# A gate pair by seven products, a layer norm on ScalarE, and low parts of weights by adding DMAs

## The chip, the core and the metric

The kernel runs on one core of a Trainium2 chip. The time is the device time of one execution in microseconds (us). Five engines work side by side, each through its own instructions in the order in which they were laid down: TensorE (PE, with its weight loads PEld), VectorE (DVE), ScalarE (ACT), GpSimd (POOL) and SyncE (SP, which here only issues DMAs). They wait for one another by semaphores. DMAs are issued by SP, by POOL and a few by ACT.

## The reference

One layer of a hybrid encoder, 512 positions of width 1024, in float32. Cut to what this case touches:

```python
n = rms_norm(h, norm_mix_pre)
proj = n @ w_in                       # columns: u 512 | v 512 | q, k, v 3 x 1536 | gates 2 x 1024
u, v = gelu(proj[:, :512]), gelu(proj[:, 512:1024])
v = (v - mean(v)) * rsqrt(var(v) + eps) * gain + bias           # layer norm over 512 channels
y_a = u * (w_spatial @ v + b_spatial)                           # 4 chunks of 128, 4 groups of channels
y_b = dilated_window_attention(q, k, v)                         # 3 head groups, mixed
g_a, g_b = sigmoid(gates + b_gate)
merged = g_a * (y_a @ w_branch_a) + g_b * (y_b @ w_branch_b)
h = h + rms_norm(merged @ w_out)
h = h + rms_norm(relu(rms_norm(h) @ w_up) ** 2 @ w_down)
```

## The kernel before

**Precision.** Every large product is made in a reduced 32-bit format (float32r). Both operands are split into a high part, which is the value rounded to that format, and a low part, which is what is left; `mm3` then adds high x high, low x high and high x low: three matmuls for one. A split of a weight (`wsplit`, `split_into`) is a copy on ACT for the high part and a subtraction on DVE or POOL for the low part.

**Seven products.** Where a product is large, the kernel uses a scheme in Strassen's manner: from a pair of 128-column weight blocks and two halves of 256 positions it makes seven products of half the contraction and half the positions, each of 4 x 3 = 12 matmuls of 128x256, where the plain way needs 2 x 8 x 3 = 48 matmuls of 128x512. The weights must first be added into sums: `seven` makes three sums on DVE (lines 339, 340, 344), splits them by `wsplit` into s12 and s34, and splits three raw blocks by `split1` (ar0, ar1, a12). The moving side (`nmov`, made early in `four_sums`) is shared by all pairs.

**Order.** The program is traced in the order of the code; a planner then orders each engine's instructions by a simulated timeline, so that instructions of neighbouring parts are interleaved. `tc.issue_after(x)` makes the instructions of a block stand behind x on x's engine. A tile with a single buffer (the pool `gapool` has one of each name) is written again only when its last reader is done.

**The stage around the change**, in the order of the code:

1. After the last attention head's scores, `token_major(COL_V, ...)` projects the gMLP values v by chunks of 128 positions. `evac_v` (line 685 on) takes each chunk from PSUM: GELU (ACT and DVE), `bn_stats` and `bn_aggr` for mean and variance on DVE, the power of -1/2 on POOL (`rstd_of`, line 96), and at line 694 one DVE instruction (v - mean) * r in place. `normed` keeps these instructions.
2. Four groups g of the first half u: the weights come in two loads (`uw`, 1024 KB each); each group is split at line 704 with the subtraction on POOL (`sub=nc.gpsimd`), multiplied (24 matmuls), put through GELU, and joined with the spatial product `pg` (line 719), which reads the normalized v. The last head's attention is interleaved (`attend_steps`).
3. The gates. With `GSTD = 1`, output block d = 0 takes the plain way: lines 793 to 799 split both gate weights and make 2 x 24 matmuls, then a sigmoid each. Blocks 1 to 7 go through `seven_pairs`, whose first `seven` stands behind the last of `normed`. Within a pair the products come as 6, (the tail of the pair before: product 4 and `after`), 1, 5, 2, 7, 3. X takes products 1 and 2, Y 6, 7 and 4, Z 5 and 3; `p1`, `z5`, `u2`, `u3` are copies and sums taken between two products into one bank.
4. `branches(d)`, called for d = 0 and from `gate_after` for the rest: for br = 1 and 0 the 128-column block of `w_branch_b` and `w_branch_a` (loaded to `bw` by SP at line 760) is split into the tile `b1` or `b0`, multiplied in 12 matmuls, and weighed with the gate; then the sum is split into `mh`, `ml` for the product with w_out.

Of the kernel before, what the change touches and what calls it, by code (L numbers as in the profile page):

```python
# [10 lines left out]
F32 = mybir.dt.float32  # L11
F32R = mybir.dt.float32r
AF = mybir.ActivationFunctionType
ALU = mybir.AluOpType
PSUM = bass.MemoryType.PSUM

P = 128
S = 512
D = 1024
KD = D // P  # L20
# [8 lines left out]
COL_U, COL_V = 0, GW  # L29
# [7 lines left out]
def block_kernel(ctx: ExitStack, tc: tile.TileContext, x, norm_mix_pre, w_in, b_gate, ln_v_gain, ln_v_bias,  # L37
                 w_spatial, b_spatial, w_branch_a, w_branch_b, w_out, norm_mix_post, norm_mlp_pre, w_up,
                 w_down, norm_mlp_post, ident_c, rope_c, mask_c, perm_c, out):
    nc = tc.nc  # L40
    x, out, w_in, w_up, w_down, w_out = x[0], out[0], w_in[0], w_up[0], w_down[0], w_out[0]
    w_branch_a, w_branch_b, w_spatial = w_branch_a[0], w_branch_b[0], w_spatial[0]
# [10 lines left out]
    wpool = pool(wstack, "wpool", bufs=3)  # L53
# [15 lines left out]
    def wsplit(raw, pl=None, bufs=None, tag="w", sub=None):  # L69
        pl = pl or wpool  # L70
        shape = list(raw.shape)
        hi = pl.tile(shape, F32R, name="hi", tag=tag + "hi", bufs=bufs)
        lo = pl.tile(shape, F32R, name="lo", tag=tag + "lo", bufs=bufs)
        nc.scalar.activation(hi, raw, AF.Copy)  # L74
        (sub or nc.vector).tensor_tensor(lo, raw, hi.bitcast(F32), op=ALU.subtract)  # L75
        return hi, lo

    def split_into(hi, lo, src, sub=nc.vector):
        nc.scalar.activation(hi, src, AF.Copy)  # L79
        return sub.tensor_tensor(lo, src, hi.bitcast(F32), op=ALU.subtract)  # L80
# [131 lines left out]
    scaled, hi, lo, _ = norm_x(blocks[0], xts[0], rs[0])  # L212
# [12 lines left out]
    for i in range(4):  # L225
        if i + 1 < 4:
            _, hi, lo, turned = norm_x(blocks[i + 1], xts[i + 1], rs[i + 1])
# [34 lines left out]
    A, B = slice(0, 256), slice(256, 512)  # L262
# [39 lines left out]
    def fcols(wap, c0, nk, n, raw=None):  # L302
        return wap[:, c0:c0 + n].rearrange("(k p) c -> p k c", p=P)
# [45 lines left out]
    def product(n, ps, w, moving, first):  # L349
        (wh, wl), (bh, bl) = w[n], moving[n]  # L350
        for j in range(KH):
            for i, (a, b) in enumerate(((wh, bh), (wh, bl), (wl, bh))):
                nc.tensor.matmul(ps, a[:, j], b[:, j], start=first and not (j or i), stop=(j == KH - 1 and i == 2), skip_group_check=True)  # L353

    def seven_pairs(n, weights, moving, banks, snap, two, rows, evac, after):
        tail = None
        for i in range(n):
            c2, c1 = rows(i)
            w = weights(i)
            Y, Z, X = banks()  # L360
            product(6, Y, w, moving, True)
            if tail:
                tail()
            product(1, X, w, moving, True)
            p1, z5, u2, u3 = snap("p1", two), snap("z5", 1), snap("u2", 1), snap("u3", 1)
            nc.scalar.activation(p1, X, AF.Copy)
            nc.vector.tensor_tensor(u2, Y, p1, op=ALU.add)
            product(5, Z, w, moving, True)
            nc.scalar.activation(z5, Z, AF.Copy)
            product(2, X, w, moving, False)  # L370
            evac(i, c1[:, A], X)
            product(7, Y, w, moving, False)
            nc.vector.scalar_tensor_tensor(u3, Y, -1.0, p1, op0=ALU.mult, op1=ALU.subtract)
            product(3, Z, w, moving, False)
            nc.vector.tensor_tensor(c1[:, B], Z, u2, op=ALU.add)
            nc.vector.tensor_tensor(c2[:, B], u3, z5, op=ALU.subtract)

            def tail(i=i, w=w, Y=Y, p1=p1, c2=c2):
                product(4, Y, w, moving, False)
                nc.vector.scalar_tensor_tensor(c2[:, A], Y, -1.0, p1, op0=ALU.mult, op1=ALU.subtract)  # L380
                after(i)
        tail()
# [301 lines left out]
    normed = []  # L684

    def evac_v(c, ps):
        v = vln[:, c]
        gelu2(ps, v)
        st6 = small.tile([P, 6], F32, name="st6")
        nc.vector.bn_stats(st6, v)  # L690
        mv = small.tile([P, 2], F32, name="mv")
        nc.vector.bn_aggr(mv, st6)
        r = rstd_of(mv[:, 1:2], 1.0, 4.0 * EPS)
        normed.append(nc.vector.tensor_scalar(v, v, mv[:, 0:1], r, op0=ALU.subtract, op1=ALU.mult))

    token_major(COL_V, lambda n, k, c: n[:, k, ROT + c * P:ROT + (c + 1) * P], evac_v)

# [2 lines left out]
    for g2 in range(2):  # L700
        raw = wload([KD, 2 * P], lambda r: [(r, fcols(w_in, COL_U + g2 * 2 * P, KD, 2 * P))], "uw")
        for j in range(2):
            g = 2 * g2 + j
            wh, wl = wsplit(raw[:, :, j * P:(j + 1) * P], sub=nc.gpsimd)
            ps = psA.tile([P, S], F32, name="pf", tag="acc" if g else "T", bufs=4 if g else 1)
            for k in range(KD):
                ins = mm3(ps, (wh[:, k], wl[:, k]), (nhn[:, k], nln[:, k]), k == 0, k == KD - 1)
                if k % 4 == 3 and steps:
                    with tc.issue_after(ins.ins):
                        if next(steps, 0) == 0:  # L710
                            steps = None
            u = gpool.tile([P, S], F32, name="u", bufs=2)
            gelu2(ps, u)
            if g == 0:
                with tc.issue_after(ins.ins):
                    spatial_weights()
            pg = psA.tile([P, 4, P], F32, name="pg", tag="acc", bufs=4)
            for c in range(4):
                nc.tensor.matmul(pg[:, c], vln[:, c, g * P:(g + 1) * P], wst[:, g], start=True, stop=True)
            t = gpool.tile([P, 4, P], F32, name="sv")  # L720
            nc.vector.scalar_tensor_tensor(t, pg, cols[:, 16 + g:17 + g], sbias[:, g:g + 1].to_broadcast([P, 4, P]), op0=ALU.mult, op1=ALU.add)
            tf = t.rearrange("p c t -> p (c t)")
            nc.vector.scalar_tensor_tensor(tf, tf, 0.5, u, op0=ALU.mult, op1=ALU.mult)
            split_into(yah[:, g], yal[:, g], tf)
# [8 lines left out]
    gapool = pool(gp, "gapool")  # L733
    gs, rawb = {}, {}

    GSTD = 1

    w7 = w_down.rearrange("(c j h p) d -> c h p j d", p=P, h=2, j=4)
    halves = [slice(0, 512), slice(512, 1024)]
# [11 lines left out]
    def gate_rows(i):  # L751
        d = i + GSTD
        gs[d] = gapool.tile([P, 2, S], F32, name="gs")
        return gs[d][:, 0], gs[d][:, 1]
# [9 lines left out]
    def gate_weights(i):  # L764
        raw = gate_raw(i + GSTD)
        with nullcontext() if i else tc.issue_after(normed[-1].ins):
# [5 lines left out]
    def gate_evac(i, dst, X):  # L772
        d = i + GSTD
        nc.scalar.activation(dst, X, AF.Sigmoid, bias=cols[:, d:d + 1])

    def gate_after(i):
        d = i + GSTD
        nc.scalar.activation(gs[d][:, 1, B], gs[d][:, 1, B], AF.Sigmoid, bias=cols[:, d:d + 1])
# [3 lines left out]
    def branches(d):  # L782
        g = gs.pop(d)
        for br in (1, 0):
            bhl = gapool.tile([P, 2, 4, P], F32R, name=f"b{br}")
            split_into(bhl[:, 0], bhl[:, 1], rawb[d][:, br])
            yh, yl = ((yah, yal), (ybh, ybl))[br]
            pb = feature_tile(bhl[:, 0], bhl[:, 1], 4, yh, yl, "Ty"[br])
            nc.vector.tensor_tensor(g[:, 1 - br], pb, g[:, 1 - br], op=ALU.mult)
        nc.vector.tensor_tensor(g[:, 0], g[:, 0], g[:, 1], op=ALU.add)  # L790
        split_into(mh[:, d], ml[:, d], g[:, 0])

    for d in range(GSTD):
        g2 = gate_rows(d - GSTD)
        raw = gate_raw(d)
# [51 lines left out]
    for k0 in range(0, KD, 2):  # L847
        raw = wload([2, D], lambda r: [(r, w_out[k0 * P:(k0 + 2) * P].rearrange("(k p) c -> p k c", p=P))], "wow")
        for j in range(2):
            wos.append(wsplit(raw[:, j]) if k0 + j < 3 else wsplit(raw[:, j], wopool, tag="wo"))  # L850
    raw = wload([KD, 2 * P], lambda r: [(r, fcols(w_up, 0, KD, 2 * P))], "upw")
# [28 lines left out]
    for t in range(4):  # L880
# [18 lines left out]
        r = rstd_of(ss, 1.0 / D)  # L899
# [30 lines left out]
    def hid_of(f):  # L930
        return hid[f // 8][:, f % 8]
# [10 lines left out]
    for i in range(1, NSTD):  # L942
        raw = raw_up(i)
        for j in range(2):
            wh, wl = split_back(raw[:, :, j * P:(j + 1) * P], [KD, P])
# [13 lines left out]
    A, B = slice(0, 256), slice(256, 512)  # L959
# [37 lines left out]
    moving = {1: nb[0, 0], 2: nb[1, 0], 3: nb[1, 1], 4: nt[4], 5: nt[1], 6: nt[2], 7: nt[3]}  # L997
# [11 lines left out]
    def snap(name, bufs=1):  # L1009
        return upool.tile([P, 256], F32, name=name, bufs=bufs)  # L1010

    tail = None
    for i in range(NSTD, KF // 2):
# [3 lines left out]
        c2, c1 = hid_of(f), hid_of(f + 1)  # L1017
        w = prep(i)
        Y, Z, X = half_bank("acc"), half_bank("acc"), half_bank("tp")
# [3 lines left out]
        p1, z5, u2 = snap("p1", 2), snap("z5"), snap("u2")  # L1023
# [11 lines left out]
        u3 = c2[:, 256:]  # L1035
# [7 lines left out]
        def tail(w=w, Y=Y, p1=p1, c2=c2, f=f):  # L1043
# [13 lines left out]
    X, W, Y, Z = [[accs[t][hf].rearrange("p (b d) -> p b d", d=256) for t in ts]  # L1057
                  for ts, hf in (((0, 1), 0), ((0, 1), 1), ((2, 3), 0), ((2, 3), 1))]
# [50 lines left out]
    for c in range(NC):  # L1109
        h = h_split(a11[c], c == 0)  # L1110
        with ExitStack() as order:
# [3 lines left out]
            w = w_split(pairs(block(c, 0, 0)))  # L1115
# [107 lines left out]
    for t in range(2):  # L1223
        with tc.issue_after(final.ins) if final else nullcontext():
            for j in range(4):
                wh, wl = w[j // 2]
                final = acc3(Y[t], (hh[:, j, tsl[t]], hl[:, j, tsl[t]]), (wh[:, j % 2], wl[:, j % 2]), False, j == 3)
        weighed(Y[t], None, 0, sums[2 + t][:, 1:2])
        r = rstd(2 + t)
# [50 lines left out]
```

## Time and profile before

| | us |
|---|---|
| median of three runs | 778.27 |
| lowest and highest run | 777.62, 779.86 |
| the profiled execution | 779.39 |
| its span, first to last instruction | 777.6 |
| PE busy in the span | 768.1 |
| DVE busy | 606.4 |
| ACT busy | 460.5 |
| POOL busy | 90.6 |

The median is what the change is measured by; the profiled execution is one of its own, with 1.8 us outside the span. Busy time of PE is the union of its matmuls, whose ends are modelled: an instruction's own duration (389 ns for a 128x512 matmul) contains the overlap with the next, and the pace of matmuls is read from the distance of their starts. In a row of the timeline the columns are the start, the duration, engine, line, operation, output<-input, and in brackets the idle time before it with what ended it. The granted clock of PE was 0.998.

### The profile page before, as it was taken

To read this page: it belongs to the slowest core of one execution; us is meant where nothing else is said; L and a number is where in the kernel's file an instruction comes from. 1 tells how busy PE (TensorE), PEld (TensorE's weight loads), DVE (VectorE), ACT (ScalarE), POOL (GpSimd) and SP (SyncE) were. 2 spreads that over 40 slices of the span, in tenths; PEclk is the share of its full clock that TensorE was granted. 3 is DMA by queue.
4 is the path that set the end of the run, shared out by engine and by line. 5 is a ranking of instruction groups with operands and counts; after the bars stand their busy time and mean duration, and the time that the engine had idled before them with its cause. 6 is when DMAs were issued, how large, how long until landed. Compare 5 with 4: busy or idle time off the path is not lost.

```text
span 777.6 us, 12381 instructions
## 1 busy us (share of the span) xinstructions
PE 768.1 (99%) x4859; PEld 693.7 (89%) x4859; DVE 606.4 (78%) x974; ACT 460.5 (59%) x751; POOL 90.6 (12%) x125
## 2 busy tenths in 40 slices
PE   8999999999999999999999999999999999999996
PEld 6888999999998888999998899999999988888885
DVE  6785589888883888868756569998888699978785
ACT  5442558978777546545544457566666766655670
POOL 2301200010103400000000210011211100203010
PEclk9999999999999999999999999999999999999999
DMA  9733844253454633433546414469999988979702
GB/s 299 257 112 108 217 109 109 55 144 101 125 175 84 201 82 83 109 82 105 144 159 203 150 69 147 152 200 285 200 277 220 240 303 312 198 248 215 214 1 109
DMA packets 104749, 128.30 MB, mean 165 GB/s; under 512 B 3265, under 2 KB 75233, under 8 KB 103794
## 3 DMA queue, kind: packets, MB, share of 16 engines
q1 hardware_dynamic: 83920, 83.50, 34.2%
q0 software_dynamic: 20480, 43.61, 23.5%
q8 instruction: 38, 0.62, 0.3%
q10 hardware_dynamic: 290, 0.40, 0.1%
q14 instruction: 21, 0.17, 0.1%
HBM read 117.53 MB, written 26.74 MB: 186 GB/s over the span
## 4 chain that ended last, share of the span: by engine, by line
PE 64%; issue 0%; DVE 0%; ACT 0%; POOLq 0%; POOL 0%; DVEq 0%; ACTq 0%
PE pacc L1003 13%; PE pd L1095 6%; PE pd L1094 6%; PE pd L1096 6%; PE pgacc L353 6%; PE ptp L1003 5%; PE pf L86 3%; PE pf L85 3%; PE pf L84 3%; PE pgS L353 3%; PE pd L84 2%; PE pd L86 2%; PE pd L85 2%; PE pu L85 1%; PE pu L86 1%; PE pu L84 1%
## 5 line engine op out<-in xcount | busy, mean ns | idle before, releaser
L1095 PE MATMUL pd<-hl,hhl 128*128 128x512 f32 x224 | 87.2, 389 | 0.0
L1096 PE MATMUL pd<-hl,hhl 128*128 128x512 f32 x224 | 87.0, 389 | 0.0
L1094 PE MATMUL pd<-hl,hhl 128*128 128x512 f32 x224 | 84.7, 389 | 0.0
L1003 PE MATMUL pacc<-nt,hl 128*128 128x256 f32 x504 | 66.1, 279 | 0.0
L1003 PEld LDWEIGHTS pacc<-nt,hl 128*128 128x128 f32 x504 | 62.0, 188 | 0.1
L74 ACT ACTIVATE hi<-s 128x1024 fp32r<-128x1024 f32 x32 | 33.8, 1058 | 29.5 <-DVE s L340 7.9
L1096 PEld LDWEIGHTS pd<-hl,hhl 128*128 128x128 f32 x224 | 42.1, 188 | 8.8
L1094 PEld LDWEIGHTS pd<-hl,hhl 128*128 128x128 f32 x224 | 42.0, 188 | 8.8
L1095 PEld LDWEIGHTS pd<-hl,hhl 128*128 128x128 f32 x224 | 42.0, 188 | 8.6
L75 DVE TENSOR_TENSOR lo<-s,hi 128x1024 fp32r<-128x1024 f32 x32 | 39.1, 1223 | 10.0 <-ACT hi L74 9.8
L80 DVE TENSOR_TENSOR hl<-dnw,hl 128x1024 fp32r<-128x1024 f32 x32 | 38.4, 1222 | 8.6 <-ACT hl L79 8.6
L79 ACT ACTIVATE hl<-s 128x1024 fp32r<-128x1024 f32 x28 | 29.4, 1057 | 26.1 <-DVE s L986 18.8
L79 ACT ACTIVATE hl<-dnw 128x1024 fp32r<-128x1024 f32 x32 | 33.0, 1053 | 19.3 <-DMA dnw<-in_w_down_dram 10.1
L1003 PE MATMUL pacc<-n,hl 128*128 128x256 f32 x336 | 44.1, 279 | 0.0
L1003 PEld LDWEIGHTS pacc<-n,hl 128*128 128x128 f32 x336 | 41.4, 188 | 0.0
L353 PE MATMUL pg<-nt,hi 128*128 128x256 f32 x216 | 39.8, 281 | 0.0
L80 DVE TENSOR_TENSOR hl<-s,hl 128x1024 fp32r<-128x1024 f32 x28 | 34.2, 1221 | 5.2 <-ACT hl L79 5.2
L84 PE MATMUL pf<-nh,hi 128*128 128x512 f32 x96 | 37.9, 395 | 0.0
L86 PE MATMUL pf<-nh,lo 128*128 128x512 f32 x96 | 37.7, 393 | 0.0
L85 PE MATMUL pf<-nl,hi 128*128 128x512 f32 x96 | 37.7, 392 | 0.0
L85 PE MATMUL pv<-lo,nh 128*128 128x512 f32 x96 | 37.5, 391 | 0.0
L84 PE MATMUL pv<-hi,nh 128*128 128x512 f32 x96 | 37.2, 394 | 0.0
(385 smaller groups left out, 2274.6 us busy)
## 6 DMA issues: line engine op xcount, KB each, us to landing
upw<-in_w_up_dram SPq DMA_DIRECT2D x16, 1024.0 KB, 6.2
qkw<-in_w_in_dram SPq DMA_DIRECT2D x24, 512.0 KB, 5.2
dnw<-in_w_down_dram SPq DMA_DIRECT2D x12, 1024.0 KB, 6.9
gw<-in_w_in_dram SPq DMA_DIRECT2D x16, 512.0 KB, 5.2
t3d<-in_w_down_dram POOLq DMA_DIRECT2D x8, 1024.0 KB, 8.9
t1d<-in_w_down_dram POOLq DMA_DIRECT2D x8, 1024.0 KB, 9.3
slab<-in_w_in_dram SPq DMA_DIRECT2D x6, 1024.0 KB, 12.5
tsum<-in_w_down_dram POOLq DMA_DIRECT2D x6, 1024.0 KB, 9.7
```

Of the source, the lines that this page charges most:

```text
L74: nc.scalar.activation(hi, raw, AF.Copy)
L75: (sub or nc.vector).tensor_tensor(lo, raw, hi.bitcast(F32), op=ALU.subtract)
L79: nc.scalar.activation(hi, src, AF.Copy)
L80: return sub.tensor_tensor(lo, src, hi.bitcast(F32), op=ALU.subtract)
L84: nc.tensor.matmul(ps, ah, bh, start=start, stop=False)
L85: nc.tensor.matmul(ps, ah, bl, start=False, stop=False)
L86: return nc.tensor.matmul(ps, al, bh, start=False, stop=stop)
L353: nc.tensor.matmul(ps, a[:, j], b[:, j], start=first and not (j or i), stop=(j == KH - 1 and i == 2), skip_group_check=True)
L1003: ins = nc.tensor.matmul(ps, a[:, j], b[:, j], start=first and not (j or m), stop=(j == KH - 1 and m == 2), skip_group_check=True)
L1094: nc.tensor.matmul(ps, ah, bh, start=start, stop=False, skip_group_check=True)
L1095: nc.tensor.matmul(ps, ah, bl, start=False, stop=False, skip_group_check=True)
L1096: return nc.tensor.matmul(ps, al, bh, start=False, stop=stop, skip_group_check=True)
```

## The change

Four edits.

- `GSTD` becomes 0: block d = 0 also goes through `seven_pairs` (eight pairs instead of seven), and the loop of the plain way is empty.
- `seven_pairs`: in the first pair, which has no tail of a pair before it, the order of the products becomes 1, 2, 6, 5, 7, 3, with the bank X emptied after product 2. The other pairs keep theirs.
- `evac_v`: the instruction (v - mean) * r on DVE is replaced by a negation of the mean (128x1, DVE) and two activations over the chunk on ACT, v - mean and then times r. `normed` now keeps the negations.
- A new helper `dma_split` is used for the four gMLP first-half weights and the sixteen branch weights: the high part by a copy on ACT, then the negated high part into the low tile by a second copy on ACT, then a DMA issued by POOL that adds the weight itself, from DRAM, to that tile. It replaces the subtraction (on POOL for the first, on DVE for the second).

```diff
+    def dma_split(raw, src, hi=None, lo=None):
+        if hi is None:
+            hi = wpool.tile(list(raw.shape), F32R, name="hi", tag="whi")
+            lo = wpool.tile(list(raw.shape), F32R, name="lo", tag="wlo")
+        nc.scalar.activation(hi, raw, AF.Copy)
+        nc.scalar.activation(lo, hi.bitcast(F32), AF.Copy, scale=-1.0)
+        nc.gpsimd.dma_start(lo, src, accum_op=ALU.add)
         return hi, lo
...
             Y, Z, X = banks()
-            product(6, Y, w, moving, True)
+            p1, z5, u2, u3 = snap("p1", two), snap("z5", 1), snap("u2", 1), snap("u3", 1)
             if tail:
+                product(6, Y, w, moving, True)
                 tail()
             product(1, X, w, moving, True)
-            p1, z5, u2, u3 = snap("p1", two), snap("z5", 1), snap("u2", 1), snap("u3", 1)
             nc.scalar.activation(p1, X, AF.Copy)
+            if not tail:
+                product(2, X, w, moving, False)
+                evac(i, c1[:, A], X)
+                product(6, Y, w, moving, True)
             nc.vector.tensor_tensor(u2, Y, p1, op=ALU.add)
             product(5, Z, w, moving, True)
             nc.scalar.activation(z5, Z, AF.Copy)
-            product(2, X, w, moving, False)
-            evac(i, c1[:, A], X)
+            if tail:
+                product(2, X, w, moving, False)
+                evac(i, c1[:, A], X)
...
-        normed.append(nc.vector.tensor_scalar(v, v, mv[:, 0:1], r, op0=ALU.subtract, op1=ALU.mult))
+        normed.append(nc.vector.tensor_scalar(mv[:, 0:1], mv[:, 0:1], -1.0, None, op0=ALU.mult))
+        nc.scalar.activation(v, v, AF.Identity, bias=mv[:, 0:1])
+        nc.scalar.activation(v, v, AF.Copy, scale=r)
...
-            wh, wl = wsplit(raw[:, :, j * P:(j + 1) * P], sub=nc.gpsimd)
+            wh, wl = dma_split(raw[:, :, j * P:(j + 1) * P], fcols(w_in, COL_U + g * P, KD, P))
...
-    GSTD = 1
+    GSTD = 0
...
-            split_into(bhl[:, 0], bhl[:, 1], rawb[d][:, br])
+            dma_split(rawb[d][:, br], fcols((w_branch_a, w_branch_b)[br], d * P, 4, P), bhl[:, 0], bhl[:, 1])
```

More of the change, by code (lines that the diff above doesn't have):

```diff
@@ L75, in wsplit @@
         (sub or nc.vector).tensor_tensor(lo, raw, hi.bitcast(F32), op=ALU.subtract)
+        return hi, lo
+    def dma_split(raw, src, hi=None, lo=None):
[5 more added lines that the diff above has]
+        nc.gpsimd.dma_start(lo, src, accum_op=ALU.add)
         return hi, lo
```

## The prediction

> **What bounds the kernel.** I read the page's busy times first, then the chain of waits, then the waits of PE alone.
>
> ```profile
> PE 768.1 (99%) x4859; PEld 693.7 (89%) x4859; DVE 606.4 (78%) x974; ACT 460.5 (59%) x751; POOL 90.6 (12%) x125
> PE 64%; issue 0%; DVE 0%; ACT 0%; POOLq 0%; POOL 0%; DVEq 0%; ACTq 0%
> ```
> ```profile
> PE pt L192 <- DVE w0lo L207: 1.9, 1, 1.9
> PE idle L160 <- POOL neghalf L60: 1.0, 1, 1.0
> ```
>
> PE is busy 99% of the span, the chain holds nothing else of weight, and PE's two listed waits (2.9 us) lie at the kernel's start. The stage of the change, in windows (length, then busy time of PE, PEld, DVE, ACT, POOL; clock; DMA share):
>
> ```profile
> 265.00:275.00 10.00, 9.89 (x58) 8.33 (x57) 9.26 (x18) 2.14 (x3) 2.76 (x3) 1.00 0.41 120
> 275.00:285.00 10.00, 10.00 (x50) 8.43 (x49) 8.34 (x12) 3.96 (x6) 0.00 (x0) 1.00 0.03 6
> 285.00:290.00 5.00, 5.00 (x27) 4.28 (x27) 4.16 (x6) 2.07 (x3) 0.00 (x0) 1.00 1.13 299
> 355.00:371.00 16.00, 16.00 (x115) 15.02 (x114) 12.70 (x20) 8.18 (x15) 0.00 (x0) 1.00 0.44 115
> ```
>
> The reader is to see PE filled to the last digit, except for 0.11 us at 265 to 275, at full clock. So time falls only by fewer matmuls or by that 0.11 us; work taken from DVE or POOL is worth nothing by itself. And time rises by every hole that a late operand makes.
>
> **Part 1, block 0 by seven products.** Two pairs of rows of PE's timeline give the pace of each way: the first matmul of block 0 and the first after it; the last product 4 of the stage and the first matmul after it.
>
> ```profile
> 286.54 0.48 PE L84 MATMUL pf<-nh,hi 128*128 128x512 f32 x1
> 297.51 0.40 PE L353 MATMUL pgacc<-nt,hi 128*128 128x256 f32 x2
> ...
> 409.73 1.56 PE L353 MATMUL pgacc<-nt,ar 128*128 128x256 f32 x12
> 411.14 0.39 PE L84 MATMUL pd<-hi,mh 128*128 128x512 f32 x1
> ```
>
> The plain way takes 297.51 - 286.54 = 10.97 us for 48 matmuls. A product takes 411.14 - 409.73 = 1.41 us, so seven take 9.87. Gain: **1.10 us**. That is all PE can win here, 0.14% of the time.
>
> What it adds is DVE work: two splits of 1024 columns go, the sums, two splits of sums and three splits of raw blocks come.
>
> ```profile
> L75 DVE TENSOR_TENSOR lo<-gw,hi x2: 1215/1216/1217, 275.4 to 282.2; 128x1024 fp32r<-128x1024 f32 x2
> L339 DVE TENSOR_TENSOR s<-gw x7: 1218/1225/1226, 270.9 to 372.4; 128x1024 f32<-128x1024 f32 x7
> L340 DVE TENSOR_TENSOR s<-s,gw x7: 680/685/695, 272.2 to 374.5; 128x512 f32<-128x512 f32 x7
> L80 DVE TENSOR_TENSOR ar<-gw,ar x14: 682/689/694, 296.7 to 395.2; 128x512 fp32r<-128x512 f32 x14
> ```
>
> New for block 0: 1.22 + 2 x 0.69 (sums) + 2 x 1.22 + 3 x 0.69 (splits) = 7.1 us, less 2 x 1.22 = 2.4 of the plain way: 4.7 us more, wanted between the last normalization (270.5) and about 292, where product 7 would start (286.5 + 4 x 1.41). DVE's idle time from 275 to 290 is 1.66 + 0.84 = 2.5 us, and part 2 frees about 2 us more, so the work fits, barely. Product 1 wants only ar0, and product 2 only a12, neither of them a sum; this is what the new order of the first pair gives.
>
> That order puts product 2 straight behind product 1 in the same bank, with the copy p1 on ACT between them. Nearest rows, the last matmul of a product 1 and its copy:
>
> ```profile
> 301.50 0.28 PE L353 MATMUL pgS<-nh,ar 128*128 128x256 f32 x1
> 301.82 0.39 ACT L366 ACTIVATE p<-pgS 128x256 f32<-128x256 f32 x1 [2.06 <-PE pgS L353]
> ```
>
> From 301.50 to the copy's end at 302.21 are 0.71 us; less the matmul's own pace of 0.12, a hole of 0.59 if PE has nothing else; none if matmuls of product 6 or of `pg` fill it, as they do in all seven pairs. I take 0.3, because the only certain filler, product 6, waits for sums that are later than ar0.
>
> **Part 2, layer norm on ACT.** DVE's rows for the second and the last chunk, PE's last `pg` of group 0, and POOL's rows:
>
> ```profile
> 264.33 2.62 DVE L694 TENSOR_SCALAR vln<-vln,mv,rs_out 128x512 f32<-128x512 f32 x1 [1.58 <-POOL rs_out L96]
> 270.48 0.55 DVE L694 TENSOR_SCALAR vln<-vln,mv,rs_out 128x512 f32<-128x512 f32 x1 [0.67 <-POOL rs_out L96]
> 271.08 0.49 PE L719 MATMUL pg<-wst,vln 128*128 128x128 f32 x2
> ...
> 264.27 2.39 POOL L75 TENSOR_TENSOR lo<-uw,hi 128x1024 fp32r<-128x1024 f32 x1
> 269.90 0.55 POOL L96 TENSOR_TENSOR rs_out<-rs_in,neghalf 128x1 f32<-128x1 f32 x1 [1.66 <-DVE rs_in L90]
> 402.93 0.11 POOL L101 MEMSET tedge<- 128x8 f32 x1 [132.48 <-PE pf L86]
> ```
>
> The last normalization ends at 271.03 and PE's `pg` starts at 271.08: here PE loses its 0.11 us. One DVE instruction of 0.55 becomes two ACT ones of about 0.63 (ACT's 128x512 row in part 3), of which only the second waits for POOL's power; ACT is busy 2.14 of these 10 us. I credit the **0.1 us**. ACT is fuller from 255 to 264; a late chunk there is priced below. The 2.62 us row began while POOL subtracted; without that subtraction I count it as 0.55, 2.1 us of DVE's room, none of it PE's. The Trainium skill, SBUF — State Buffer, "Who interferes with whom", has DVE and GpSimd lock each other out of a shared port pair for whole instructions. These rows agree (2.62 beside 2.39, against 0.55 alone); by the rule alone the sum stays as it is.
>
> **Part 3, adding DMAs.** A group of u costs ACT a second copy of 1.06 us, a branch block one of 0.63, and POOL an issue. No row shows an adding DMA of 256 or 512 KB in 512-byte rows. From above: adding DMAs into SBUF, which ran beside a busy DMA. From below: plain ones issued by POOL.
>
> ```profile
> tsum<-in_w_down_dram POOLq DMA_DIRECT2D x6, 1024.0 KB, 9.7
> v0s<-v0d POOLq DMA_DIRECT2D x4, 512.0 KB, 5.1
> v12s<-v12d POOLq DMA_DIRECT2D x8, 256.0 KB, 5.3
> tend<-in_w_down_dram POOLq DMA_DIRECT2D x4, 512.0 KB, 11.8
> bw<-in_w_branch_a_dram SPq DMA_DIRECT2D x8, 256.0 KB, 4.8
> L315 POOL DMA_DIRECT2D v12s<-v12d x8: 747/757/797, 82.8 to 251.9; - x8
> L74 ACT ACTIVATE hi<-uw x4: 1042/1058/1062, 240.6 to 260.4; 128x1024 fp32r<-128x1024 f32 x4
> 254.45 0.39 PE L86 MATMUL pf<-nh,lo 128*128 128x512 f32 x1
> ```
>
> I take 6 us to landing (5.1 to 11.8): size and source rows are those of v0s and v12s, and the DMA share is 0.44, not 0.9. The room in the gates' stage, from block 5, and at the last block:
>
> ```profile
> 362.25 0.63 ACT L79 ACTIVATE b<-bw 128x512 fp32r<-128x512 f32 x1 [0.50 <-PE pf L86]
> 374.75 0.40 PE L84 MATMUL pf<-ybh,b 128*128 128x512 f32 x1
> ...
> 393.15 0.63 ACT L79 ACTIVATE b<-bw 128x512 fp32r<-128x512 f32 x1 [1.41 <-PE pf L86]
> 399.94 0.40 PE L84 MATMUL pf<-ybh,b 128*128 128x512 f32 x1
> ```
>
> Tile `b1` is free at 362.25 and wanted at 374.75, 12.5 us later. The chain is 2 x 0.63 + 0.76 + 6 = 8.0, so it is hidden, up to a landing of 10.5 us. What stands behind a POOL issue that waits for ACT is only POOL's later issues: POOL's rows in part 2 show it without work from 270.45 to 402.93. For u the first group is the tight one: its copy, the first of the four of line 74, starts at 240.6 and ends at 241.65, a second at 242.7, landing at 242.7 + 0.8 + 6 = 249.5, wanted at 254.45 (third matmul). Hidden. DVE's 1.38 us per block that go are worth nothing to PE.
>
> **Sum.** -1.10 - 0.10 + 0.30 = -0.9. Against its own execution 779.39 would become 778.5; that execution is 1.1 us above the median, so on the median 778.27 - 0.9 = **777.4**.
>
> **Rivals.** (a) *The start of pair 0 runs late.* `bw` for block 0 came late:
>
> ```profile
> 235.64 48.77 SPq L66 DMA_DIRECT2D gw<-in_w_in_dram  x6
> 284.62 0.86 SPq L760 DMA_DIRECT2D bw<-in_w_branch_a_dram  x1
> 293.64 1.28 ACT L798 ACT_TABLE_LOAD   x1
> ```
>
> Landing (4.8) at 289.4 to 290, two copies, issue and 6 us put the low part at 298; PE reaches it after seven products at 286.5 + 9.9 = 296.4, later if product 6 and 1 of pair 1 stand between. DVE is nearly full there, so sums can be late too. Price 2 to 4, taken as 3: 780.4. Against it: both branch halves and the next pair's products can fill. The sigmoid of pair 0 now comes near the last tanh; a load of 1.28 us before each change of function would lengthen ACT's part of this by up to 2.6. The Trainium skill, ScalarE: Activation LUTs, "Table sets: the hidden batching unit", lists tanh beside sigmoid in one set, by which no load back would be needed; no row here shows that order.
> (b) *The first u low parts are late* (landing at 11.8: 255.3, 0.9 after it is wanted), or a POOL issue waiting for ACT holds the powers of the norm behind it: 1 to 3, taken as 2: 779.4.
> (c) **Slower:** *every block waits for its adding DMA.* It decides at a landing of 10.5 us. At tend's 11.8 a block loses 1.3, and eight lose 10: 788. At the last block, where `b1` was free at 393.15 and wanted at 399.94, less is enough, once. Against it: only the busiest part of the kernel shows such landings.
> (d) *More than the count*: the planner's new order also closes holes that the modelled ends hide, 2.5 us more: 774.9. Nothing in the rows speaks for it.
>
> **How the numbers follow.** Forecast 0.60, (a) 0.20, (b) 0.07, (c) 0.08, (d) 0.05. What a measurement can tell from no change is about 0.3%, 2.33 us: below 775.94 is faster, above 780.60 slower. Faster is (d): 0.05. Slower is (c), nearly half of (a) and little of (b): 0.17. The rest, 0.78, is within. The range runs from 1.0 below the forecast, the spread of the runs before, to 780.8: it holds the forecast, (b), and over half of (a), about 0.8.
>
> **What would show it.** Right: PE has 36 matmuls more of 128x256 by line 353's count (84 in place of 48 of 128x512), its busy time falls by about 1, and PE's waits show nothing above 0.5 us between 240 and 415. For (a): a PE wait near 287 to 302 on DVE, ACT or a DMA. For (c): PE waits on a DMA into b, once per block. What would make the forecast wrong most cheaply is a landing above 10.5 us.

## The result and the profile after

The changed kernel takes **791.03 us** (median of 4 runs, 790.53 to 792.05) beside 778.90 for the kernel before in the same session: ratio 1.0164, interval 1.0152 to 1.0177. It is slower by 12 us, where 777.4 was forecast.

The page after, busy times and chain of waits by engine:

```profile
PE 772.7 (98%) x4895; PEld 695.5 (88%) x4895; DVE 599.0 (76%) x969; ACT 480.6 (61%) x785; POOL 108.1 (14%) x141
PE 85%; DMA 6%; DVE 4%; ACT 3%; issue 2%; SPq 0%; POOL 0%; POOLq 0%; DVEq 0%; ACTq 0%
```

The 36 additional matmuls are there (4895 - 4859), but PE's busy time rose by 4.6 us instead of falling by 1, and DMA, DVE and ACT now hold parts of the chain. The place is found with a landmark, the first matmul of the product with w_out, in the timeline of PE after:

```profile
422.23 0.39 PE L93 MATMUL pd<-hi,mh 128*128 128x512 f32 x1
```

Before it stood at 411.14. So it stands 11.1 us later, of a span that grew by 788.8 - 777.6 = 11.2: the loss lies ahead of this matmul, and behind it nothing changed. The first matmul of the first half u (`pf<-nh,hi`) stood at 253.99 before and stands at 252.69 after. So the stretch from there to w_out lost 12.4 us, and what comes ahead of it ran 1.3 us faster in this execution than in that of before, all of it ahead of 95 us, far from the changed code. PE's list of waits after (us in total, times, longest), for 250 to 430 us; before, the list of this stretch was empty:

```profile
PE pf L95 <- DMA b<-in_w_branch_a_dram: 2.8, 2, 2.1
PE pf L93 <- ACT b L82: 1.8, 1, 1.8
PE pgacc L362 <- DVE u L387: 0.9, 1, 0.9
PE pgacc L362 <- DVE sv L737: 0.6, 1, 0.6
PE pf L95 <- DMA b<-in_w_branch_b_dram: 0.5, 1, 0.5
PE pg L735 <- ACT vln L710: 0.5, 1, 0.5
PE pgS L362 <- ACT ar L88: 0.4, 1, 0.4
PE pgS L362 <- DVE ar L89: 0.3, 1, 0.3
```

That is 7.8 us. Windows of the stage after (the prediction's columns; PE's granted clock is the third figure from the right):

```profile
265.00:275.00 10.00, 10.00 (x61) 8.75 (x60) 6.53 (x10) 5.41 (x10) 0.97 (x1) 1.00 1.00 214
...
285.00:290.00 5.00, 4.35 (x38) 4.18 (x38) 4.59 (x7) 3.43 (x5) 0.00 (x0) 1.00 0.00 0
290.00:300.00 10.00, 7.50 (x55) 6.80 (x54) 6.73 (x11) 5.02 (x11) 0.23 (x1) 0.96 0.60 158
300.00:310.00 10.00, 10.00 (x65) 9.51 (x65) 6.94 (x12) 7.30 (x12) 2.37 (x2) 0.87 0.88 181
...
380.00:390.00 10.00, 8.41 (x49) 6.82 (x48) 5.14 (x9) 2.26 (x4) 0.00 (x0) 1.00 0.34 74
...
400.00:410.00 10.00, 7.93 (x42) 6.64 (x41) 4.25 (x6) 5.17 (x9) 1.36 (x2) 0.83 0.75 228
```

Two things are to be seen: PE has holes at 285 to 300, at 380 to 390 and at 400 to 410, and behind the two longest (1.8 us at 296 and 2.1 at 402) its clock is below 1. Windows of 1 us behind the first long hole (length, PE's busy time, clock):

```profile
299.00:300.00 1.00, 1.00 (x8) 0.60 0.00 0
300.00:301.00 1.00, 1.00 (x6) 0.50 0.03 11
301.00:302.00 1.00, 1.00 (x7) 0.50 0.75 217
302.00:303.00 1.00, 1.00 (x8) 0.70 0.86 244
```

PE is full but runs at half clock for about 3.4 us: 0.40 + 0.50 + 0.50 + 0.30 = 1.7 us lost. The hole at 402 costs the same again (405 to 409). So busy time rose: it contains the 3.4 us that the slow clock took. Waits 7.8 + clock 3.4 - the count's gain of 1.1 = 10.1 of the 12.4 us. No row names the other 2.3. Some of it is in the way that the list counts: a hole begins there at the modelled end of the matmul before it, which for a 128x512 matmul (0.39 us, starts 0.23 apart) is 0.16 us late; nine holes would hide 1.4 us (an estimate from these two figures).

How the first long hole arises, in the timeline after, in order along SP, ACT and PE:

```profile
260.09 31.72 SPq L66 DMA_DIRECT2D gw<-in_w_in_dram  x4
...
292.03 0.69 SPq L776 DMA_DIRECT2D bw<-in_w_branch_a_dram  x1
...
297.44 0.63 ACT L82 ACTIVATE b<-bw 128x512 fp32r<-128x512 f32 x1 [3.56 <-DMA bw<-in_w_branch_a_dram]
...
298.13 0.50 PE L93 MATMUL pf<-yah,b 128*128 128x512 f32 x1 [1.80 <-ACT b L82]
```

SP issues in order. The branch weights of block 0 stand behind a gw load that waits for a free buffer until 291.8, so they land at 297.4 and PE stands. Before, they stood behind the same six gw loads (the row at 235.64 in the prediction), but the last pair of these got its buffer 7.4 us earlier, at 283.4 in place of 290.8: there it was released by the split of a plain gate weight, here by the split of a sum of the first pair. So the branch load was issued at 284.62. The second long hole, on ACT, POOL, SP and PE:

```profile
390.27 0.62 ACT L82 ACTIVATE b<-bw 128x512 fp32r<-128x512 f32 x1
...
391.91 1.40 POOL L84 DMA_DIRECT2D b<-in_w_branch_a_dram  x1
...
392.82 11.95 SPq L66 DMA_DIRECT2D wow<-in_w_out_dram  x3
...
404.24 0.50 PE L95 MATMUL pf<-yah,b 128*128 128x512 f32 x1 [2.07 <-DMA b<-in_w_branch_a_dram]
```

The high part of branch a of block 6, the last but one, is copied at 390.27, the adding DMA issued at 391.91, loads of w_out start a microsecond later, and the low part lands 12.3 us after its issue. The tile's summary after gives the least, the median and the longest landing:

```profile
DMA to landing us min/median/max: 4.2/6.0/12.3
```

### The profile page after: what moved, and what is told of

Its sections match the earlier page's. It is cut to its first block, busy times and chain, and to the rows that moved or that the text cites. A ratio compares the mean times of both kernels' runs of the same rounds, so it can differ in the third digit from the quotient of the medians.

```text
span 788.8 us, 12513 instructions
## 1 busy us (share of the span) xinstructions
PE 772.7 (98%) x4895; PEld 695.5 (88%) x4895; DVE 599.0 (76%) x969; ACT 480.6 (61%) x785; POOL 108.1 (14%) x141
## 4 chain that ended last, share of the span: by engine, by line
PE 85%; DMA 6%; DVE 4%; ACT 3%; issue 2%; SPq 0%; POOL 0%; POOLq 0%; DVEq 0%; ACTq 0%
PE pacc L1019 12%; PE pg L362 11%; PE pd L1111 5%; PE ptp L1019 5%; PE pd L1112 5%; PE pd L1110 5%; PE pgacc L362 4%; PE pv L94 4%; PE pv L95 4%; PE pv L93 4%; PE pf L95 4%; PE pf L93 4%; PE pf L94 4%; PE pgS L362 2%; PE pd L94 2%
## 5 line engine op out<-in xcount | busy, mean ns | idle before, releaser
L74 ACT ACTIVATE hi<-s 128x1024 fp32r<-128x1024 f32 x34 | 35.8, 1057 | 42.0 <-DVE s L349 20.7
L75 DVE TENSOR_TENSOR lo<-s,hi 128x1024 fp32r<-128x1024 f32 x34 | 41.5, 1223 | 9.0 <-ACT hi L74 8.7
L95 PE MATMUL pv<-hi,nl 128*128 128x512 f32 x96 | 36.9, 391 | 0.0
L1100 DVE TENSOR_TENSOR hhl<-hid,hhl 128x1024 fp32r<-128x1024 f32 x24 | 29.3, 1221 | 9.4 <-ACT hhl L1099 9.2
L362 PE MATMUL pgacc<-nt,hi 128*128 128x256 f32 x192 | 35.4, 283 | 0.6 <-DVE sv L737 0.6
## 6 DMA issues: line engine op xcount, KB each, us to landing
slab<-in_w_in_dram SPq DMA_DIRECT2D x6, 1024.0 KB, 11.2
```

The costliest lines, as they stand in the source:

```text
L95: return nc.tensor.matmul(ps, al, bh, start=False, stop=stop)
```

## The experiments

Three theories stood at first. **A**: two sources, the start of the first pair and the branches' adds. **B**: the adding DMAs are the whole loss. **C**: ScalarE is too full.

**Each part alone.** Every edit was put by itself into the kernel before: `GSTD = 0` with the new product order; the branches by `dma_split`; the first half by `dma_split`; the layer norm on ScalarE.

```diff
-    GSTD = 1
+    GSTD = 0                                     # seven_alone, with the new order
-            split_into(bhl[:, 0], bhl[:, 1], rawb[d][:, br])
+            dma_split(rawb[d][:, br], fcols((w_branch_a, w_branch_b)[br], d * P, 4, P), bhl[:, 0], bhl[:, 1])   # branch_add_alone
```

> Only the first edit pair: block 0 by seven products and the new order of the first pair; layer norm on DVE and all low parts by subtraction, as before. Theory A (the loss has two sources, the start of pair 0 and the adding DMAs of the branch blocks): the holes at the start of pair 0 stay, 3.8 us in the changed kernel between 288 and 298, and about 1.7 us of a halved clock after the longest, less 1.1 us of matmuls: 3 to 5 us above before. Theory B (the adding DMAs are the whole loss): 1 us below before. Theory C (ACT is too full by the layer norm and the extra copies): 1 us below before.

> Only the sixteen branch weights' low parts by adding DMAs, on the kernel before (block 0 the plain way). Theory A: holes at products of b with a DMA as releaser, as at 317, 383 and 404 in the changed kernel, 4.9 us together and 1.7 us of halved clock: 5 to 7 us above before. Theory B: the whole loss, 11 to 13 us above before. Theory C: little, 0 to 2 us, since only 16 copies of 0.63 us go to ACT.

> Only the four gMLP first-half weights' low parts by adding DMAs, on the kernel before. Theories A and B: within 0.5 us of before, because these low parts landed 5 us and more before they were wanted. Theory C: 1 us or more above before.

> Only the layer norm on ACT, on the kernel before. Theories A and B: within 0.7 us of before (a hole of 0.5 us at the spatial product, as at 263 in the changed kernel, in place of 0.1). Theory C: 3 us or more above before, with holes in the gMLP stage.

Measured beside 778.32 for before: seven_alone 782.00 (ratio 1.0053, 1.0037 to 1.0070), branch_add_alone 790.31 (1.0157, 1.0142 to 1.0173), u_add_alone 777.04 (0.9987, 0.9977 to 0.9996), ln_alone 777.28 (0.9989, 0.9979 to 0.9998), the last two a little further below than any theory had it. C falls. A names the right two parts but gave the branches half their price; B has their price but not the first pair. The four together make 3.7 + 12.0 - 1.3 - 1.0 = 13.4 against 12.1 measured: nearly a sum. PE's hole of seven_alone, in its timeline, is the one of the whole change, without any adding DMA:

```profile
297.17 0.50 PE L84 MATMUL pf<-yah,b 128*128 128x512 f32 x1 [2.11 <-ACT b L79]
```

and PE's waits in branch_add_alone, 290 to 420 us:

```profile
PE pf L95 <- DMA b<-in_w_branch_a_dram: 4.8, 3, 2.4
PE pf L95 <- DMA b<-in_w_branch_b_dram: 2.1, 2, 1.7
PE pgacc L362 <- DVE u L382: 1.8, 2, 1.0
```

The waits for the low parts themselves are 6.9 us; the third row is another path. `u` stands on DVE behind the gate sum `s`, and DVE's waits in branch_add_alone say for what `s` waited:

```profile
DVE s L348 <- DMA gw<-in_w_in_dram: 18.2, 5, 6.2
```

In the kernel before, the row for the same stretch is:

```profile
DVE s L339 <- DMA gw<-in_w_in_dram: 2.7, 4, 1.3
```

**Is it the traffic, or the work on ScalarE?** `ghost` and `ghost2` leave the low parts on DVE and add, per branch, a POOL DMA of the same 256 KB (an adding one from block 1 on) into a DRAM tile that nobody reads. `neg_dve` makes the second copy on ACT but no DMA. There are sixteen DMAs (4 MB) and sixteen copies, where the expectations say 3 MB and twelve.

```diff
             split_into(bhl[:, 0], bhl[:, 1], rawb[d][:, br])
+            seen = nc.gpsimd.tensor_copy(warm[:1, :1], ...)      # ghost2: one element of bhl's high part
+            with tc.issue_after(seen.ins):
+                nc.gpsimd.dma_start(ghost[br], fcols((w_branch_a, w_branch_b)[br], d * P, 4, P), ...)
```

```diff
-            split_into(bhl[:, 0], bhl[:, 1], rawb[d][:, br])
+            nc.scalar.activation(bhl[:, 0], rawb[d][:, br], AF.Copy)
+            nc.scalar.activation(bhl[:, 1], bhl[:, 0].bitcast(F32), AF.Copy, scale=-1.0)
+            nc.vector.tensor_tensor(bhl[:, 1], rawb[d][:, br], bhl[:, 1].bitcast(F32), op=ALU.add)
```

> The kernel before with all low parts by VectorE as they were, and beside each branch's subtraction one more 256 KB POOL DMA of the same weights, issued after the same high copy, into a DRAM tile that nobody reads. Theory L (the 12.0 us of the branch adds are the wait for their landing): nobody waits for these, 777.5 to 780. Theory T (traffic: the extra 3 MB and the POOL issues delay the loads of gw and wow, on which VectorE and then TensorE wait): 784 to 791, with VectorE again waiting some 18 us on gw. Theory K (ScalarE has too little room for the negating copies): as L, 777.5 to 780.

> The kernel before with the branches' low parts as raw + (-hi): ScalarE makes the negated copy as in the change, VectorE adds where it subtracted; no DMA is added. Theory K (the twelve more copies on ScalarE and the chain through it): most of the 12.0 us, 785 to 791. Theories L and T: no DMA, so 778 to 780.

> As ghost, but the unread 256 KB DMA of each branch stands in POOL's order behind a one-element copy of the branch's high part, so that it runs in the block itself, where the adding DMA ran; SP's order of loads is that of the kernel before. Theory L (TensorE waits for the landing of the low parts, and SP's loads in another order): nobody waits for these, 778 to 779.5. Theory T (their traffic delays gw, bw and wow): VectorE waits 10 us or more on gw (2.7 before), TensorE behind it 2 to 6 us, 780 to 787.

`ghost` gave 782.56 (1.0060, 1.0039 to 1.0081) and says nothing on the question. The tile's summary shows its DMAs at the kernel's start, where the planner had put them, not in the gates:

```profile
L791 POOL DMA_DIRECT2D ghost<-in_w_branch_b_dram x8: 812/1194/1371, 2.1 to 62.7; - x8
```

`ghost2` has them in place (300.8 to 397.9 us) and takes 778.40, ratio 0.9998 (0.9989 to 1.0008). `neg_dve` takes 778.32, ratio 0.9998 (0.9988 to 1.0007). So neither the 256 KB transfers beside the others nor the copies cost anything by themselves. In ghost2 the unread DMAs land after

```profile
DMA to landing us min/median/max: 4.6/6.7/8.5
```

and DVE waits for gw 5.4 us in all, not 18. Traffic and copies alone are ruled out, with the limit that these DMAs land in DRAM and not in SBUF; what is left is that somebody waits for the landing, and that the loads then stand in another order.

**Lateness without a DMA.** `branch_pool` puts the subtraction on POOL; `branch_pool_late` adds four copies of the low part in place behind it.

```diff
-            split_into(bhl[:, 0], bhl[:, 1], rawb[d][:, br])
+            split_into(bhl[:, 0], bhl[:, 1], rawb[d][:, br], nc.gpsimd)
+            for _ in range(4):                                    # branch_pool_late
+                nc.gpsimd.tensor_copy(bhl[:, 1], bhl[:, 1])
```

> The kernel before with the branches' low parts subtracted by POOL instead of VectorE: no DMA, no second copy on ScalarE, a low part some 1.3 us after its high one (VectorE 0.7, the adding DMA 0.6 + 1.3 + 4 to 12). Theory L with the room that the trace of before has (a block's low part is wanted several us after its high one): 777.5 to 779. If even 1.3 us comes too late, or POOL's place in line does: 780 or more.

> branch_pool with four copies of each low part in place behind POOL's subtraction, so that it is ready some 6 us (estimate: 1.3 + 4 x 1.2) after its high part, as late as behind an adding DMA (0.6 + 1.3 + 5 to 8), with no byte more from HBM and nothing on ScalarE. Theory L (lateness alone, through the one buffer of b: a late low part holds TensorE, TensorE then frees b later, and the next high copy is late): TensorE waits for b in several blocks, 781 to 788. Theory M (lateness hurts only together with the traffic that stretches the landing to 8 to 12 us at the loads of gw and wow): 777.5 to 779.5.

`branch_pool` takes 778.42, ratio 0.9998 (0.9989 to 1.0007): a low part that POOL makes in 1.30 us, where DVE takes 0.69, costs nothing. `branch_pool_late` takes 828.39 (1.0642, 1.0623 to 1.0661), far outside both theories. It is not a clean test: VectorE's rows grew too (some of its 128x512 additions and subtractions took 1.09 us, the others 0.69), and PE's longest waits are for VectorE, with only 3.4 us named for b:

```profile
PE pgacc L353 <- DVE gs L375: 15.9, 4, 6.7
...
PE pf L86 <- POOL b L788: 3.4, 1, 3.4
```

It doesn't decide. A repeat of ghost2 for its landings was spoilt:

> ghost2 once more, one look, for the landing of the unread DMAs beside the loads of gw and wow: median 5 to 7 us by theory M and L alike; the time 778 to 779.

This single run took 1861.53 us, with TensorE slow from end to end (a 128x512 matmul of line 1100: 680 ns in the mean, 389 before), beside 778.42 for the kernel before on the same chip. Nothing is drawn from it.

**Which adds cost.** The adding DMAs in blocks 2 to 6 only; for branch b only; for branch a only.

```diff
+            if 2 <= d <= 6:                                       # add_mid; "if br" in add_b_only, "if not br" in add_a_only
                 dma_split(rawb[d][:, br], fcols((w_branch_a, w_branch_b)[br], d * P, 4, P), bhl[:, 0], bhl[:, 1])
+            else:
+                split_into(bhl[:, 0], bhl[:, 1], rawb[d][:, br])
```

> branch_add_alone with the adds in blocks 2 to 6 alone; blocks 0, 1 and 7 subtract on VectorE. Theory S (the adds lose at the two ends: bw of block 0 lands late, block 0's low parts with it, which holds back block 1; and at the last block the landing meets the loads of wow and takes 12.6 us): what is left are the two waits behind gw, 778 to 781. Theory E (each block has too little room, as the forecast's rival of a late landing had it): five of the eight blocks keep their part of 12.0, 7.5: 784 to 788.

> branch_add_alone with the adds for branch b (the first of a block) alone, eight DMAs in place of sixteen. Sum of the waits of branch_add_alone's trace that name branch b or stand behind gw (2.1 + 1.8): 781 to 783. Theory C (two adds of one block in flight at once beside bw and gw stretch each other's landing): alone they land in about 5 and cost nothing, 778 to 780.

> branch_add_alone with the adds for branch a (the second of a block) alone. Sum of the waits that name branch a, the half clock behind the last, and those behind gw (4.8 + 1.7 + 1.8): 785 to 788. Theory C: 778 to 780.

add_mid takes 785.27 (1.0080, 1.0065 to 1.0095), add_b_only 782.93 (1.0041, 1.0026 to 1.0056), add_a_only 782.52 (1.0044, 1.0027 to 1.0060). add_b_only came as its sum had it; add_a_only stayed under its sum of 785 to 788. S falls: the middle blocks carry 6.7 of the 12.0 us, close to their five eighths. (The hole beside the loads of w_out, which S put at the last block, is block 6's, by the order of the copies; add_mid keeps that add, and there PE waited nothing for it.) E has the number, but not the mechanism: in add_mid PE waits little for b and mostly for DVE's `u`:

```profile
PE pgacc L362 <- DVE u L382: 2.8, 2, 2.1
PE pf L95 <- DMA b<-in_w_branch_a_dram: 0.9, 1, 0.9
```

and these rows of add_mid's timeline (SP, then DVE) show what `s`, ahead of `u`, waited for:

```profile
352.49 0.37 SPq L769 DMA_DIRECT2D bw<-in_w_branch_a_dram  x1
...
354.40 1.32 SPq L66 DMA_DIRECT2D gw<-in_w_in_dram  x2
...
364.61 1.22 DVE L348 TENSOR_TENSOR s<-gw 128x1024 f32<-128x1024 f32 x1 [6.35 <-DMA gw<-in_w_in_dram]
```

In the kernel before, in the same views:

```profile
351.42 0.99 SPq L66 DMA_DIRECT2D gw<-in_w_in_dram  x2
353.22 0.37 SPq L760 DMA_DIRECT2D bw<-in_w_branch_a_dram  x1
...
357.44 1.23 DVE L339 TENSOR_TENSOR s<-gw 128x1024 f32<-128x1024 f32 x1 [0.83 <-DMA gw<-in_w_in_dram]
...
366.63 0.99 SPq L66 DMA_DIRECT2D gw<-in_w_in_dram  x2
```

Before, gw goes first and `s` starts 6.0 us after its issue. In add_mid both high copies of a block come close together (350.66 and 351.85 on ACT; 346.82 and 351.18 before), which frees `bw` together; its loads go ahead of gw, the two adds are in flight as well, and `s` starts 10.2 us after gw's issue. The gw loads go round in a loop: the next is issued when VectorE has read the last use of a buffer (SP's row for gw names `ar`). The loop took 366.63 - 351.42 = 15.2 us before, with `s` waiting 0.8 us in it already: VectorE had no slack there. TensorE had some, since ghost2's 5.4 us of such waits cost nothing. Theory C falls in its number (neither half alone is free) but not wholly: 4.4 and 4.0 make 8.4, less than the 12.0 of both. That the order of the loads, and not the landing of b alone, makes this part of the loss is read from these rows; no run had the adds with gw first.

**The first pair.** `seven_bw_pool` is seven_alone with block 0's branch loads on POOL's queue; `seven_old_bw` also takes back the order of the products; `no_add_bw_pool` is the whole change without the branches' adds and with those loads on POOL; `u_ln` keeps of the change only the first half's adds and the layer norm.

```diff
-            nc.sync.dma_start(rawb[d][:, br], ...)
+            (nc.sync if d else nc.gpsimd).dma_start(rawb[d][:, br], ...)
```

> seven_alone with block 0's two branch loads on POOL's queue, past the gw loads that hold SP's. Theory A (the start of pair 0 waits for bw behind the third gw load): the hole of 2.26 at 297 goes, and with it the 4 us at half clock behind it (some 1.9): 782.0 - 2.26 - 1.9 = 777.8; 777 to 778.5. Rival R (the hole is ScalarE's order, with the split of the two-gate sum behind the last gMLP split): the hole stays, 781 to 783.

> The changed kernel without the branches' adds and with block 0's branch loads on POOL's queue: what is left are the seven products for block 0, the layer norm on ScalarE and the first half's adds. Theory A with the lone results summed: 777.8 - 1.3 - 1.0 = 775.5; 775 to 777.5. Rival R: 779 to 781.

> seven_bw_pool with the products in the order of before (6 first, then 1 and 2), so that only the count and the place of bw are changed. Theory O (the new order costs what is left of seven_bw_pool's loss, 1.5 us): 777 to 778. Rival P (the seven products of the first pair want sums and copies from VectorE and ScalarE at the seam, where the plain block had its weights ready): the waits of 0.3 to 0.7 at 287 to 293 stay, 779 to 781.

> The changed kernel with the first gate pair plain, in the old order, and the branches' low parts by VectorE: only the first half's adds and the layer norm on ScalarE stay. If the two lone gains (1.3 and 1.0) add up: 776; if they are the same gain (a start of the blocks that comes earlier) or noise: 777 to 778. Slower than 778.5 would say that they hinder one another.

seven_bw_pool takes 779.90 (1.0018, 1.0008 to 1.0027). The long hole and the half clock are gone, as A had it, but only 2.1 of the expected 4.2 us came back. PE's waits, all that is left of them from 280 to 420:

```profile
PE pgacc L353 <- DVE sv L726: 0.7, 1, 0.7
PE pgacc L353 <- DVE u L371: 0.4, 1, 0.4
PE pgS L353 <- ACT ar L79: 0.4, 1, 0.4
PE pgS L353 <- DVE ar L80: 0.3, 1, 0.3
```

These are 1.8 us, 1.4 of them at the seam (288 to 293), where the gMLP's last values and the first pair's splits want VectorE and ScalarE together. They outweigh the 1.1 us that the count gives; the rest of its 1.5 us over the kernel before isn't named by a row. seven_old_bw, 780.29 (1.0020, 1.0011 to 1.0029), has the same four waits: rival P, and the order of the products in the source decides nothing. no_add_bw_pool takes 779.99 (1.0022, 1.0012 to 1.0031), 4.5 above A's sum and in the range of R, though the long hole that R keeps isn't there: without the branches' adds and with early branch weights 1.6 of the 12.1 us are left.

`u_ln` takes **777.39** (0.9981, 0.9972 to 0.9989), the lowest ratio of all, and its trace shows no wait of PE from 200 to 420. It is the part of the change worth keeping: 1.35 us, less than the two lone gains (1.3 and 1.0) together, so these don't add. Where the 1.35 us come from is not shown: PE's idle time from 250 to 430 was only 0.11 us before, and of the 2.3 us between the two profiled spans (777.6 and 775.3) 1.6 lie ahead of 95 us, far from the changed code (the first `pf<-nh,hi` of all stands at 94.35 and at 92.77).

## Why the prediction was wrong

**The failed step** is in part 3: "so it is hidden, up to a landing of 10.5 us", and with it that the branches' adds cost nothing. Alone they cost 12.0 us. The typical landing was sized rightly: 6 taken, 6.0 measured. Wrong was what the chain of 8.0 us was set against, in two ways.

The room was read in one wide block. Block 5 has 12.5 us, but at the last block the prediction's own rows leave 6.8, less than the chain, and the sum counts nothing for it. In block 1 of the kernel before, a row that the prediction didn't look up, the tile `b1` is free at 308.31 and its low part is wanted 5.4 us later:

```profile
308.31 0.63 ACT L79 ACTIVATE b<-bw 128x512 fp32r<-128x512 f32 x1 [0.42 <-PE pf L86]
313.69 0.40 PE L86 MATMUL pf<-ybh,b 128*128 128x512 f32 x1
```

In branch_add_alone PE waits 1.75 and 2.10 us for the two low parts of block 1, and in add_b_only, which keeps the order of before at the end, 2.33 for the last block. In block 6 of the whole change the landing itself passed 10.5: 12.3 us, beside the loads of w_out, and a hole of 2.07 (2.41 in branch_add_alone). Waits for low parts are 6.9 of the 8.7 us of PE waits in branch_add_alone from 290 to 420.

The rest of the schedule was taken to stay as it was. The edit brought copies and loads into another order, and gw came later: DVE waited for it 2.7 us in all before, another row that the prediction didn't look up, and 18 with the adds, and PE behind it for `u`. That they share the DMA engines is not enough for this: in ghost2, with as many DMAs in flight but the loads in the order of before, the gw loads land after 5.3 us (median; 5.2 before, 6.9 in branch_add_alone) and the time stays. How the 12.0 us divide between the late low parts and the order of the loads stays open.

**Part 1.** The count was right (36 more matmuls). The copy between products 1 and 2 (0.30) never showed: the planner ran the products in an order of its own. "The work fits, barely" failed: PE waits for VectorE and ScalarE at this seam even with bw early (1.4 us), which eats the gain of 1.10.

**Rival (a)** was right in place and mechanism: the hole stands at 296.3 to 298.1, inside "near 287 to 302", on the chain from bw. Its price of 3 was near seven_alone's 3.7, but for other reasons: bw was taken at the issue of the trace of before (284.62), while the gw load in front of it waits longer for its buffer in the change (292.03), and the hole brings the clock with it. Nothing of the hole came from the adds. **Rival (c)** was right in sign and size (788 against 790.3 for this part alone), wrong in its condition: no landing above 10.5 is needed in each block; a block with less room, or a later gw, is enough. The two were priced as alternatives; both happened, and they add.

**Part 2** held only without the seven products for block 0: the hole at `pg` is closed in the traces of ln_alone (0.1% faster, 0.9979 to 0.9998) and u_ln, but in the whole change it became 0.52 us, waiting for ACT. The adds for u are hidden, as forecast, and rival (b) is out (no wait of PE there). The load of an activation table between tanh and sigmoid, for which (a) left up to 2.6 us, did not come: the sigmoids stayed behind the last tanh, as before.

**Not in the prediction at all**: the half clock behind a hole of about 2 us, which nearly doubles its price: 1.7 us more, twice.

## What to carry to other kernels

Before a DMA takes the place of an engine's instruction, look at the room of its result in every block, not in one, and at every load of the same stretch that somebody already waits for: the edit can move it behind others. Where a load's queue is in order, read what stands ahead of it in the changed program, not its old issue time. In a kernel that keeps TensorE full, a hole of about 2 us can cost nearly twice its length.

## What the runs showed of the hardware

**The clock falls behind short holes, not each time.** The granted clock went to 0.50 for about 3.4 us behind six PE holes of 1.80 to 2.41 us (in the gates' stage of after two, and one each of seven_alone, branch_add_alone, add_mid and add_b_only). It stayed at 1 behind three, of 1.75 and 2.10 us in branch_add_alone and 2.09 in add_a_only. Windows of 1 us in add_mid, behind a hole of 2.13 us (364.70 to 366.83):

```profile
366.00:367.00 1.00, 0.17 (x1) 1.00 0.00 0
...
368.00:369.00 1.00, 1.00 (x7) 0.50 0.00 0
```

and in add_a_only, behind one of 2.09 us (364.71 to 366.80) in the same place:

```profile
366.00:367.00 1.00, 0.20 (x1) 1.00 0.00 0
...
368.00:369.00 1.00, 1.00 (x7) 1.00 0.00 0
```

The Trainium skill, TensorE: Matmul & The Clock Gate, "What's actually happening", has a free-running window of about 3.4 us, after an idle one of which the clock is halved. The length of the slow stretch agrees with it, and a window that runs free would let the same hole have both outcomes; but the holes of about 2 us, which were enough here, are shorter than the page's idle window.

**An adding DMA costs POOL more than a plain one.** Its issue takes 1.28 us for 256 KB (the plain ones of 256 KB 0.76; in ghost2, for the same weights into DRAM, 0.68 to 0.70 for the two plain ones and 1.05 to 1.41 for the adding ones). In the tile's summary after:

```profile
L84 POOL DMA_DIRECT2D b<-in_w_branch_a_dram x8: 1273/1286/1401, 299.8 to 409.9; - x8
```

The Trainium skill, DMA: Bandwidth & Descriptors, "Anatomy of one DMA", fits a DMA from POOL by 2.0 us + bytes / 436 GB/s, an estimate of 2.6 us for 256 KB. The measured landings of 4.2 to 12.3 us don't agree: among the loads of this stage that figure is no guide.
